# Making 22 products of the gate projections ahead of their phase, with four smaller edits, in a hybrid retention and attention layer

## The chip, the cores and the metric

One core of a Trainium2 chip runs the whole layer. The metric is device time in microseconds (us) of one execution; lower is better. TensorE (PE) multiplies matrices, VectorE (DVE), ScalarE (ACT) and GpSimd (POOL) work on tiles of 128 partitions, SyncE (SP) issues most of the DMAs. PSUM, where TensorE leaves its results, has eight banks of 512 fp32 numbers per partition.

## The reference

One layer over a sequence of 1024 tokens behind 16 meta tokens, width 1024, all in fp32:

```python
u = _rms_norm(h, pre_w)
z = u @ w_in                      # 60 column tiles of 128
rq, rk, rv, rg, aq, ak, av, ag, gr, ga = _split_in(z)
# branch A: 4 heads (key 128, value 256), chunks of 128, forward and backward scan
o_r = _bidirectional_retention(rot(rq), rot(rk), rv, lg_f, lg_b)
y_r = (group_norm(o_r) * ret_nw * silu(rg)) @ w_rb
# branch B: 8 heads in 2 groups, window of 128 to each side, 16 meta keys, one sink logit a head
#   m = max(max(s), sink); p = exp(s - m) / (sum(exp(s - m)) + exp(sink - m))
o_a = _windowed_sink_attention(rot(aq), rot(ak), av, sink)
y_a = (o_a * silu(ag)) @ w_ab
out = (sigmoid(gr) * y_r + sigmoid(ga) * y_a) @ w_o
return h + _rms_norm(out, post_w)
```

`rot` stands for the rotary positions, `lg_f` and `lg_b` for the logarithms of the decays. The four parts rg, ag, gr and ga are 32 column tiles, in the kernel 16 *gate units* of 256 columns.

## The kernel before

**Three matmuls for one.** Every fp32 product is made of three matmuls of a shorter format (`mm3`, L69 to L71: high by high, low by high, high by low). So each operand is split first: a copy in the short format is the high part (made by ScalarE, or by GpSimd through `pool_hi`, L74), and VectorE subtracts it for the low part (`dve_lo`, L77).

**Who sets the order.** The program is written stage by stage, with filler work between the steps of a stage. A scheduler then fixes, before the run, one order of instructions for each engine. It may lift an instruction over others that were written ahead of it, as far as its data and the buffers it takes allow; `tc.issue_after(x)` holds what is written under it behind x. Buffers come from pools in turn: a tag with n buffers hands out the next one only when the tile that had it n turns ago is done with. The tags of PSUM are `pj` (three banks, all projections), `p1` and `p2` (two each) and `p3` (one).

**The stages.**

1. *Retention* (`retention`, heads h = 0 to 3, up to about 330 us). Per head, a forward scan over chunks c = 0 to 8: `stage1` projects the values (`pv`), splits them and makes the scores, `stage2` adds up the outputs (`pa`) and the next state (`pkv`). Then a backward scan over c = 8 to 1: VectorE makes the next state `Sb`, GpSimd and VectorE split it (`Shb`, `Slb`), TensorE multiplies it with the queries (`pb`), VectorE adds this to the output `op`, normalises it (`bs`, `mv`, `rs`), and TensorE transposes it (`to`). In the backward scan each step calls `fill(KT)`, which draws eight pieces of filler; a piece is the three matmuls of one k of a projection. The filler of heads 0 to 2 is the next head's query and key projections (`gen_qk`), that of head 3 is the first keys and queries of the attention and one gate unit.
2. *Attention* (`attention`, pairs of heads hp = 0 to 3, about 330 to 590 us). Per block n of 128 queries: `stage1` makes the scores `ps` and the softmax, `stage2` transposes the probabilities `pt` and splits them, `stage3` multiplies with the values (`po`). Filler between the blocks, in amounts from the table `FILL`: the next queries, in pair 3 two gate units.
3. *Phases z, r, a, o* (`Phase`, `run`; from 589 us to the end). Four large products in Strassen's form as Winograd has it: a unit of 256 columns takes seven products in place of eight, each of 12 matmuls of 512 columns (`PROD`); sums of them give the four quarters of the unit (`POST`, `combine`). Phase z makes the gate units, r and a the two branch projections, o the output. The operands of a product are prepared six jobs ahead (`LEAD = 6`). The PSUM bank of a product goes by the table `at`: products 1, 6, 7 and 4 of a unit go one after the other through one bank X, which ScalarE copies out after each (`c1`, `u2`, `u3`), 5 and 3 share Y, 2 has Z. While a phase ends, hooks (`refill`) load and split the other operand of the next phase. Phase o ends in `last_product` and `o_tail`: the last addition, the square, the mean's power (on GpSimd) and the scaling of the last rows.

Three gate units (5, 6, 7 of `gr`) are made whole, with eight products' worth of matmuls, as filler by `gen_gate` (`N_GATE = 3`); the other 13 in phase z.

In the attention, the query block is split per block of 128 columns, high part on GpSimd. The sink enters the softmax's denominator by three small steps on a tile `es` (add, exponential, add). The values of a group are split per pair of heads, though two pairs share a group. `sums_of_x` makes differences of blocks of the normalised input, for phase z's operands T1 to T4, during pair 0, in a pool of its own. `x_to_out` copies six blocks of 128 rows of x to the output through on-chip memory, after pair 0; phase o adds to them.

Of the kernel before, what the change touches and what calls it, by code (L numbers as in the profile page):

```python
# [25 lines left out]
FILL = {**{h: (8, 8, 0, 8, 8, 8, 8, 0) for h in range(3)}, 3: (16, 16, 0, 16, 14, 10, 8, 0)}  # L26
N_GATE = 3
# [11 lines left out]
def block_kernel(ctx: ExitStack, tc: tile.TileContext, xT, x, w_in, w_rb, w_ab, w_out, vecs, dec, sink,  # L39
# [22 lines left out]

    xs_d = {n: dram.tile([4, P, 512], F32, tag=f"xs{n}", name=f"xs{n}") for n in ("T1", "T2", "T3", "T4")}
# [151 lines left out]
    def decay_table(hs):  # L215
        for h in hs:
            t = ra.tile([P, P], F32, tag="dd", bufs=2, name=f"dd{h}")
            nc.vector.tensor_scalar(t, tabt[:, 2 * P:3 * P], lg[:, 4 + h:5 + h], None, op0=ALU.mult)
            nc.vector.scalar_tensor_tensor(t, tabt[:, P:2 * P], lg[:, h:h + 1], t, op0=ALU.mult, op1=ALU.add)
            nc.scalar.activation(DT[:, h], t, AF.Exp)  # L220
# [211 lines left out]
    def retention(h, fill):  # L432
# [65 lines left out]
        def stage2(c):  # L498
# [11 lines left out]
            if "f" in kd:  # L510
                a, b = kd["f"]
                mm3(pk[:, 0:256], a[0:n], b[0:n], vh[0:n], vl[0:n], True, True)
# [104 lines left out]
    aq = {}  # L617

    wq = {}
# [37 lines left out]
    def sums_of_x(pool):  # L657

        x = {}

        def load(k):
            for i, j in ((0, 0), (0, 1), (1, 1), (1, 0)):
                x[k, i, j] = t = pool.tile([P, 512], F32, tag="xs", bufs=11, name=f"xs{i}{j}{k}")
                nc.sync.dma_start(t, xT[4 * i + k, :, NM + 512 * j:NM + 512 * j + 512])

        def make(k):
            for i, j in ((0, 0), (0, 1), (1, 1), (1, 0)):
                t = x[k, i, j]
                nc.scalar.activation(t, t, AF.Copy, scale=vec[:, 4 * i + k:4 * i + k + 1])
            for n, o, a, b in SUMS:  # L670
                nc.vector.tensor_tensor(x[k, *o], x[k, *a], x[k, *b], ALU.subtract)

        def store(k):
            for n, o, a, b in SUMS:
                nc.sync.dma_start(xs_d[n][k], x[k, *o])

        load(0)
        for k in range(6):
            if k < 3:
                load(k + 1)  # L680
            if k < 4:
                make(k)
            if 0 < k < 5:
                store(k - 1)
            yield
# [15 lines left out]
    def gen_gate(u):  # L701

        w = load_w(w_in, U_GR + u)
        for a, b in HALVES:
            for e_ in range(2):
                t = yield from proj(w, P * e_, a, b, f"pgt{u}_{a}{e_}")
                o = ra.tile([P, 512], F32, tag="m1", bufs=2, name=f"gt{u}_{a}{e_}")
                nc.vector.tensor_tensor(o, t, rbc[:, a:b], ALU.mult)
                nc.scalar.activation(o, o, AF.Tanh, scale=0.5)
                nc.sync.dma_start(tg_d[2 * u + e_, :, a - NM:b - NM], o)  # L710
                yield
# [5 lines left out]
    for h in range(NH):  # L717
        fill, drain = filler([*([gen_qk(h + 1)] if h < 3 else [gen_ak(0), gen_aq(0, 0), gen_gate(7)])])
# [4 lines left out]
        with tc.issue_after(rotated):  # L723
            retention(h, fill)
            drain()
# [29 lines left out]
    class Phase:  # L755
        def __init__(self, nm, seq, load, post, fetch=None, apart=(), early=()):
            self.nm, self.seq, self.load, self.post, self.fetch = nm, seq, load, post, fetch
            self.apart, self.early = apart, early
            self.raw, self.s, self.ops, self.u = {}, {}, {}, {}
            self.cur = None  # L760
# [18 lines left out]
        def prepare(self, u, p):  # L779
# [4 lines left out]
            if self.fetch and p in POST and u not in self.early:  # L784
                self.fetch(u, *POST[p])
# [11 lines left out]
            elif p == 6:  # L797
                t = self.s[u]
                self.split(u, 6, t)
                if u in self.early:  # L800
# [12 lines left out]
        def product(self, u, p):  # L813
# [3 lines left out]
            at = {1: "X", 6: "X", 7: "W" if u in self.apart else "X", 5: "Y", 3: "V" if u in self.early else "Y", 2: "Z",  # L817
# [26 lines left out]
        def combine(self, u, p, st):  # L844
# [15 lines left out]
            if p == 1:  # L860
                copy("c1")
            elif p == 2:
                self.post(u, 0, 0, plus(st["c1"], st["c1"], "Z"))
                done("Z")
            elif p == 6:
                copy("u2")
                if apart:
# [6 lines left out]
            elif p == 7 and not apart:  # L874
                copy("u3")
                if (self.nm, u) == last[:2]:
                    done("X")
            elif p == 3 and not early:
# [8 lines left out]
            if "u3" in st and "Y" in st and "c22" not in st:  # L887
                st["c22"] = plus(new("c5") if (self.nm, u) == last[:2] else st["u3"], st["u3"], "Y")
                self.post(u, 1, 1, st["c22"])
                if early:  # L890
# [21 lines left out]
    def refill(nm, src):  # L912
# [40 lines left out]

        if nm == "a":
# [157 lines left out]
    def o_tail(o, a):  # L1112
# [4 lines left out]
        if a:  # L1117
# [4 lines left out]
    seq += [(2, 1), (2, 5), (3, 1), (2, 6), (3, 5), (2, 2), (2, 7), (3, 6), (2, 4), (3, 7), (2, 3), (3, 2), (3, 3),  # L1122
            (3, 4)]
    gates = [U_G + u for u in range(4)] + [U_AG + u for u in range(4)] + [U_GR + u for u in range(8)]
    ph_o = Phase("o", seq, o_load, o_post, apart=(0, 1))
    steps = run([(Phase("z", sequence(16 - N_GATE, (1, 3, 2, 5, 6, 7, 4)), w_loader(w_in, gates), z_post, z_fetch,
                        early=(0, 1)),
# [6 lines left out]
    a_stack = ExitStack()  # L1134
    ap = a_stack.enter_context(tc.tile_pool(name="ap", bufs=1, reuse_waits="tile"))
# [18 lines left out]
    scored, softmax = [], []  # L1154

    def attention(hp, fill):
# [3 lines left out]
        vs = {}  # L1160
        oa = [None]
        st1, st2 = {}, {}

        def vsplit(b):
            a_ = ap.tile([P, P], R, tag="vh", bufs=4, name=f"vh{hp}_{b}")
            b_ = ap.tile([P, P], R, tag="vl", bufs=4, name=f"vl{hp}_{b}")
# [5 lines left out]
        def stage1(n):  # L1172
# [18 lines left out]
            es = ap.tile([P, 2], F32, tag="es", bufs=3, name=f"es{hp}_{n}")  # L1191
            pt = []
            for e_ in range(2):
                hd = 2 * hp + e_
                qr = aq[hp][e_, i][:, o0:o0 + P]
# [232 lines left out]
```

## Time and profile before

| | |
|---|---|
| time, median of 3 runs | 1092.71 us (1090.38 to 1093.98) |
| profiled execution | 1091.82 us, its span 1089.8 us |
| mean granted TensorE clock | 0.995 |
| TensorE (PE) busy | 1068.6 us, 98% of the span |
| TensorE's weight loads (PEld) | 922.5 us, 85%, beside the matmuls |
| VectorE (DVE) busy | 872.3 us, 80% |
| ScalarE (ACT) busy | 488.6 us, 45% |
| GpSimd (POOL) busy | 241.7 us, 22% |
| DMA | 159.45 MB, mean 146 GB/s |

"Busy" is time in which at least one instruction of the engine runs. Matmuls overlap, so a busy TensorE isn't one at its peak, and the count of matmuls in a stretch says more than its busy time. The granted clock is the share of its full speed that the throttle gave TensorE. In the rows below, "L69" is a line of the code, `pb<-Shb,qh` the tile written and the tiles read, by the names of the program; a row of a timeline has the start in us from the begin of the span, then the duration in us; a row of the groups has the count, the busy time in us and the mean of one in ns, then the idle time ahead of them with what ended it; a row of the stretches has for each engine the busy us and the number of instructions.

### The profile page before, as it was taken

The numbers are of one execution on the slowest core, as the hardware profiler recorded it, in microseconds if no ns is written. First come the engines' busy times: TensorE is split into PE (matmuls) and PEld (weight loads), VectorE is DVE, ScalarE is ACT, GpSimd is POOL, SyncE is SP. The second block draws the span as 40 slices with busy tenths as digits, with TensorE's granted clock in tenths as the row PEclk, the third lists the DMA queues.
The fourth block names the chain that finished last, engine by engine and source line by source line (L and its number), as shares of the span: only waits on it lengthen the run. The fifth ranks groups of instructions, "written<-read, shape, count | busy, mean of one in ns | idle before, by whom it ended". The sixth has DMA issues, their size and how long they took to land.

```text
span 1089.8 us, 17221 instructions
## 1 busy us (share of the span) xinstructions
PE 1068.6 (98%) x5975; PEld 922.5 (85%) x5975; DVE 872.3 (80%) x1864; ACT 488.6 (45%) x1132; POOL 241.7 (22%) x346
## 2 busy tenths in 40 slices
PE   8999999999999999999999999999999999999996
PEld 7899999998989889988887888888888788787885
DVE  7897778877955988898667975888889899767765
ACT  7241432513314544545657643454456546433442
POOL 3235324233322544445220000000000000110032
PEclk9999999998999999999999999999999999999999
DMA  7121101111114871112115663779874755779463
GB/s 289 39 79 40 55 24 59 59 40 39 63 44 144 295 277 60 59 59 68 50 49 169 238 227 120 247 240 324 276 274 140 236 185 200 235 202 336 118 116 78
DMA packets 75799, 159.45 MB, mean 146 GB/s; under 512 B 8128, under 2 KB 19904, under 8 KB 74944
## 3 DMA queue, kind: packets, MB, share of 16 engines
q1 hardware_dynamic: 71824, 151.78, 40.4%
q0 software_dynamic: 3456, 6.29, 3.7%
q8 instruction: 47, 0.77, 0.3%
q10 hardware_dynamic: 432, 0.28, 0.1%
q14 instruction: 40, 0.33, 0.1%
HBM read 105.89 MB, written 52.43 MB: 145 GB/s over the span
## 4 chain that ended last, share of the span: by engine, by line
PE 86%; DVE 5%; issue 3%; DMA 3%; POOL 2%; ACT 1%; SPq 0%; POOLq 0%; DVEq 0%; ACTq 0%
PE bz L70 8%; PE bz L69 8%; PE bz L71 8%; PE pv L69 3%; PE pv L70 3%; PE pv L71 3%; PE br L70 2%; PE bo L70 2%; PE bo L69 2%; PE bo L71 2%; PE br L69 2%; PE br L71 2%; PE ba L70 2%; PE ba L71 2%; PE ba L69 2%
## 5 line engine op out<-in xcount | busy, mean ns | idle before, releaser
L1054 POOL DMA_DIRECT2D mx_d<-c1a x4 | 3.7, 918 | 391.5 <-DVE c1a L1045 391.5
L70 PE MATMUL bz<-big,llz 128*128 128x512 f32 x208 | 82.4, 396 | 0.0
L71 PE MATMUL bz<-big,lhz 128*128 128x512 f32 x208 | 81.9, 394 | 0.0
L69 PE MATMUL bz<-big,lhz 128*128 128x512 f32 x208 | 80.8, 394 | 0.0
L69 PE MATMUL pv<-wh,big 128*128 128x256 f32 x256 | 73.6, 288 | 1.3 <-DVE m_qk L162 1.3
L70 PE MATMUL pv<-wh,big 128*128 128x256 f32 x256 | 73.4, 287 | 0.0
L71 PE MATMUL pv<-wl,big 128*128 128x256 f32 x256 | 73.2, 286 | 0.0
L69 PE MATMUL bz<-T,lhz 128*128 128x512 f32 x156 | 61.6, 395 | 0.0
L70 PE MATMUL bz<-T,llz 128*128 128x512 f32 x156 | 61.5, 395 | 0.0
L71 PE MATMUL bz<-T,lhz 128*128 128x512 f32 x156 | 61.3, 394 | 0.0
L1205 ACT ACTIVATE p<-p,nm 128x400 f32<-128x400 f32 (+1 forms) x64 | 38.3, 598 | 44.0 <-DVE nm L1203 42.3
L77 DVE TENSOR_TENSOR wl<-wr,wh 128x1024 fp32r<-128x1024 f32 x34 | 47.4, 1398 | 4.6 <-POOL wh L74 4.4
L70 PE MATMUL paq<-big,wl 128*128 128x512 f32 x128 | 51.0, 398 | 0.0
L71 PE MATMUL paq<-big,wh 128*128 128x512 f32 x128 | 50.9, 398 | 0.0
L69 PE MATMUL paq<-big,wh 128*128 128x512 f32 x128 | 50.8, 397 | 0.1
L69 PEld LDWEIGHTS pv<-wh,big 128*128 128x128 f32 x256 | 48.9, 191 | 2.1 <-DVE m_qk L162 1.5
L1217 POOL TENSOR_SCALAR p<-p,den 128x400 f32<-128x400 f32 (+1 forms) x60 | 36.0, 610 | 63.9 <-DVE den L1211 52.0
L70 PEld LDWEIGHTS pv<-wh,big 128*128 128x128 f32 x256 | 48.9, 191 | 0.1
L71 PEld LDWEIGHTS pv<-wl,big 128*128 128x128 f32 x256 | 48.9, 191 | 0.0
L69 PEld LDWEIGHTS bz<-big,lhz 128*128 128x128 f32 x208 | 39.0, 188 | 9.4
L70 PEld LDWEIGHTS bz<-big,llz 128*128 128x128 f32 x208 | 39.1, 188 | 9.3 <-DVE llz L77 0.2
L71 PEld LDWEIGHTS bz<-big,lhz 128*128 128x128 f32 x208 | 39.2, 188 | 8.9
(616 smaller groups left out, 3641.0 us busy)
## 6 DMA issues: line engine op xcount, KB each, us to landing
wr<-in_w_in_dram SPq DMA_DIRECT2D x35, 512.0 KB, 3.6
wrz<-in_w_in_dram SPq DMA_DIRECT2D x28, 512.0 KB, 5.7
tg<-tg_d SPq DMA_DIRECT2D x32, 256.0 KB, 4.7
T<-preT SPq DMA_DIRECT2D x6, 1024.0 KB, 7.5
oTr_d<-ost SPq DMA_DIRECT2D x16, 256.0 KB, 2.1
xs<-in_xT_dram SPq DMA_DIRECT2D x16, 256.0 KB, 5.5
xsT<-xs SPq DMA_DIRECT2D x16, 256.0 KB, 5.7
oTa_d<-oa SPq DMA_DIRECT2D x16, 256.0 KB, 2.1
```

What stands on the lines that cost most here:

```text
L69: nc.tensor.matmul(o, ah, bh, start=first, stop=False, **kw)
L70: nc.tensor.matmul(o, al, bh, start=False, stop=False, **kw)
L71: return nc.tensor.matmul(o, ah, bl, start=False, stop=last, **kw).ins
L77: return nc.vector.tensor_tensor(o, i, hi.bitcast(F32), ALU.subtract).ins
L1054: nc.gpsimd.dma_start(d, to, accum_op=ALU.add)
L1205: nc.scalar.activation(p[:, 0:wid], p[:, 0:wid], AF.Exp, scale=-1.0, bias=nm_[:, e_:e_ + 1], accum_out=den[:, e_:e_ + 1])
L1217: nc.gpsimd.tensor_scalar(pt[e_][:, 0:wid], pt[e_][:, 0:wid], den[:, e_:e_ + 1], 1.0, op0=ALU.mult, op1=ALU.mult)
```

## The change

* **Gates.** `gen_gate` is gone: all 16 gate units are made in phase z with seven products. Of these, product 2 of units 2 to 15 and product 3 of units 8 to 15 are made ahead by `gen_pre` as filler, 22 products of 12 matmuls; the result goes to a tensor in memory (`e_d`), and phase z loads it and adds it (`pre=PRE`).
* **Where they stand.** 16 pieces in the forward scans of heads 1, 2 and 3 (4, 4, 8, by `between`, behind the first matmuls of the state), 16 in the filler of head 3, the other 56 in the filler of pair 3.
* **Attention.** The sink is column 0 of the score tile (`raw`, 401 wide), so that the exponential's own sum takes it in; the `es` steps are gone. Queries are split by halves of 512, on ScalarE and VectorE (`split_q`). Values are split once for two pairs.
* **Sums of x** are made in pairs 1 and 2 (`sum_row`), in the tiles that weights are loaded to (`wr`). x goes to the output from memory to memory, in three DMAs of 1 MB.
* **Phase z's hooks** stand at other places, since products 2 and 3 of the last units are not in its sequence. The bank X of most units now takes product 7 sooner behind 6.
* **The last products** of phase o: (3, 7) moves behind (3, 3), which gets a bank of its own, V.
* `decay_table` takes its tile from the tag `rw` instead of `dd`.

```diff
-FILL = {**{h: (8, 8, 0, 8, 8, 8, 8, 0) for h in range(3)}, 3: (16, 16, 0, 16, 14, 10, 8, 0)}
-N_GATE = 3
+FILL = {**{h: (8, 8, 0, 8, 8, 8, 8, 0) for h in range(3)}, 3: (16, 16, 0, 14, 10, 8, 8, 0)}
+PRE = {u: (2, 3) if u > 7 else (2,) for u in range(2, 16)}
...
     def stage2(c):
...
-                mm3(pk[:, 0:256], a[0:n], b[0:n], vh[0:n], vl[0:n], True, True)
+                forward = mm3(pk[:, 0:256], a[0:n], b[0:n], vh[0:n], vl[0:n], True, True)
+                if h and c < 4:
+                    with tc.issue_after(forward):
+                        between(h // 3 + 1)
...
+    def split_q(hp, e_, i):
+        o = aq[hp][e_, i]
+        h, l = (aw.tile([P, 512], R, tag=f"aq{t}", bufs=4, name=f"aq{t}{hp}_{i}{e_}") for t in "hl")
+        nc.scalar.copy(h, o)
+        dve_lo(l, o, h)
+        aqs[hp, e_, i] = h, l
...
+    def gen_pre(u):
+        g = nc.vector.tensor_tensor
+        n = P * len(PRE[u])
+        raw = [keep.tile([P, 4, 256], F32, tag="wr", bufs=2, name=f"we{u}_{j}") for j in range(len(PRE[u]))]
+        for j, t in enumerate(reversed(raw)):
+            nc.sync.dma_start(t[:, :, 0:n], w_in[gates[u], :, 4 - 4 * j:8 - 4 * j, 0:n])
+        t = raw[-1]
+        if n > P:
+            v = t[:, :, P:n]
+            g(v, raw[0][:, :, P:n], v, ALU.add)
+            g(v, v, raw[0][:, :, 0:P], ALU.subtract)
+            g(v, t[:, :, 0:P], v, ALU.subtract)
+        h = wp.tile([P, 4, 256], R, tag="wh", bufs=4, name=f"weh{u}")[:, :, 0:n]
+        l = wp.tile([P, 4, 256], R, tag="wl", bufs=4, name=f"wel{u}")[:, :, 0:n]
+        nc.scalar.copy(h, t[:, :, 0:n])
+        dve_lo(l, t[:, :, 0:n], h)
+        for p in PRE[u]:
+            b = pj(f"pe{u}_{p}")
+            m = slice(P * (p - 2), P * (p - 1))
+            c = slice(NM + 512 * (p - 2), NM + 512 * (p - 1))
+            for k in range(4):
+                mm3(b, h[:, k, m], l[:, k, m], xh[4 + k][:, c], xl[4 + k][:, c], k == 0, k == 3, True)
+                if k < 3:
+                    yield
+            o = ra.tile([P, 512], F32, tag=f"m{p - 1}", bufs=2, name=f"e{u}_{p}")
+            nc.scalar.copy(o, b)
+            nc.sync.dma_start(e_d[u, p], o)
+            yield
...
-        fill, drain = filler([*([gen_qk(h + 1)] if h < 3 else [gen_ak(0), gen_aq(0, 0), gen_gate(7)])])
+        fill, drain = filler([*([gen_qk(h + 1)] if h < 3 else [gen_ak(0), pieces(pre, 16), gen_aq(0, 0)])])
...
-            retention(h, fill)
+            retention(h, fill, filler([pieces(pre, (0, 4, 4, 8)[h])])[0])
...
     class Phase:
...
+            made = {1: 2, 6: 3}.get(p)
+            if made not in self.pre.get(u, ()):
+                made = None
...
+            if made:
+                self.e[u, made] = gtile(f"e{u}{made}")
+                nc.sync.dma_start(self.e[u, made], e_d[u, made])
...
             if p == 1:
                 copy("c1")
+                e = self.e.pop((u, 2), None)
+                if e is not None:
+                    nc.vector.tensor_tensor(st["c1"], st["c1"], e, add)
+                    self.post(u, 0, 0, st["c1"])
+            elif p == 6 and (u, 3) in self.e:
+                st["u2"] = new("u2")
+                plus(st["u2"], self.e.pop((u, 3)), "X")
+                self.post(u, 0, 1, plus(st["u2"], st["u2"], "Y"))
...
-    seq += [(2, 1), (2, 5), (3, 1), (2, 6), (3, 5), (2, 2), (2, 7), (3, 6), (2, 4), (3, 7), (2, 3), (3, 2), (3, 3),
+    seq += [(2, 1), (2, 5), (3, 1), (2, 6), (3, 5), (2, 2), (2, 7), (3, 6), (2, 4), (2, 3), (3, 2), (3, 3), (3, 7),
             (3, 4)]
...
     def attention(hp, fill):
...
-                p = ap.tile([P, 400], F32, tag="p", bufs=4, name=f"p{hd}_{n}")
-                nc.vector.tensor_tensor_reduce(p[:, 0:wid], s[:, 0:wid], mask[:, mo:mo + wid], -SCALE,
+                if n == 0:
+                    raw[e_] = aw.tile([P, 401], F32, tag=f"raw{e_}", bufs=1, name=f"raw{hd}")
+                    nc.vector.tensor_copy(raw[e_][:, 0:1], nsink[:, hd:hd + 1])
+                p = ap.tile([P, 401], F32, tag="p", bufs=4, name=f"p{hd}_{n}")
+                nc.vector.tensor_tensor_reduce(raw[e_][:, 1:1 + wid], s[:, 0:wid], mask[:, mo:mo + wid], -SCALE,
                                                nsink[:, hd:hd + 1], ALU.add, ALU.min, nm_[:, e_:e_ + 1])
...
-            nc.vector.tensor_tensor(es, nm_, sinkc[:, 2 * hp:2 * hp + 2], ALU.add)
-            nc.scalar.activation(es, es, AF.Exp)
-            nc.vector.tensor_tensor(den, den, es, ALU.add)
...
+            if hp in (1, 2) and n in (2, 5):
+                sum_row(2 * hp - 2 + n // 3)
...
+        with tc.issue_after(stored[0]):
+            for r in (0, 4, 6):
+                nc.sync.dma_start(out[P * r:P * r + 2 * P], x[P * r:P * r + 2 * P])
```

137 lines of the change are left out of this document (58 added, 79 removed).

## The prediction

> **What bounds the kernel now.** I read the page first, then the busy time by stretches, then the timelines of TensorE and VectorE around the passages from one retention head to the next, and the last microseconds.
>
> ```profile
> span 1089.8 us, 17221 instructions
> PE 1068.6 (98%) x5975; PEld 922.5 (85%) x5975; DVE 872.3 (80%) x1864; ACT 488.6 (45%) x1132; POOL 241.7 (22%) x346
> core 0: us, PE busy (x) PEld busy (x) DVE busy (x) ACT busy (x) POOL busy (x), PEclk, DMA share, GB/s
> 630.00:660.00 30.00, 30.00 (x131) 24.29 (x130) 22.73 (x37) 14.82 (x26) 0.00 (x0) 1.00 0.61 207
> 107.00:122.00 15.00, 14.50 (x124) 14.21 (x122) 10.76 (x34) 4.99 (x18) 5.27 (x10) 1.00 0.11 37
> 255.00:260.00 5.00, 3.08 (x19) 2.20 (x18) 4.57 (x16) 2.11 (x7) 2.34 (x4) 0.93 0.17 56
> 260.00:266.00 6.00, 6.00 (x28) 5.59 (x27) 4.88 (x15) 2.47 (x8) 1.14 (x3) 0.50 0.14 45
> ```
>
> TensorE is the bound nearly everywhere. Its matmuls overlap, so their listed durations say nothing of the pace; the count does: 131 matmuls of 512 columns in 30 us are 0.229 us each. Time goes only where TensorE gets less work, or where it is made to wait. The one large hole in the middle is at 255 to 266 us (head 2 to head 3 of the retention): 19 matmuls in 5 us, then 28 in 6 us at a granted clock of 0.50. The two other passages look like the 107 to 122 row: 124 matmuls, full.
>
> **Part 1, TensorE work removed.** Before, three gate units are made whole: 3 units x 4 tiles x 8 x 3 = 288 matmuls, and 13 units x 7 products x 12 = 1092 in the Strassen-like phase z. After, all 16 units take 7 products: 1344, of which 22 products (264 matmuls) are made early and 90 products stay in phase z. That is 36 fewer, at 0.229 us: **-8.2 us**. All are full-pace matmuls in stretches where TensorE is the bound, so this is real if nothing else moves.
>
> **Part 2, the passages between retention heads.** This decides. I compared the compiled order of instructions of the two kernels on each engine.
>
> ```profile
> 103.46 0.28 PE L69 MATMUL pb<-Shb,qh 128*128 128x256 f32 x1
> 106.77 0.28 PE L69 MATMUL pb<-Shb,qh 128*128 128x256 f32 x1
> 120.07 0.28 PE L69 MATMUL pb<-Shb,qh 128*128 128x256 f32 x1
> 121.01 0.38 PE L555 MATMUL to<-ident,op 128*128 128x128 f32 x2
> 122.59 0.38 PE L69 MATMUL pkv<-vh,khf 16*128 16x256 f32 x1
> 124.74 0.39 PE L69 MATMUL pv<-wh,big 128*128 128x256 f32 x1
> 255.40 0.28 PE L69 MATMUL pb<-Shb,qh 128*128 128x256 f32 x1
> 256.59 0.36 PE L69 MATMUL pb<-Shb,qh 128*128 128x256 f32 x1
> 260.19 0.58 PE L69 MATMUL pkv<-vh,khf 16*128 16x256 f32 x1
> 263.32 0.41 PE L69 MATMUL pv<-wh,big 128*128 128x256 f32 x1
> ```
>
> The rows pb are steps of the backward scan, pkv is the first state of the next head's forward scan. In the old order the value projections pv_2 to pv_6 of head 1 (5 x 24 = 120 matmuls) stand between the steps pb_6 (103.46) and pb_1 (120.07); between 103.46 and 106.77 are 28 matmuls, 0.118 us each, so the cover is 14.2 us. In the new order they are gone from there. The early product `pe` takes its PSUM bank (tag `pj`, three banks) in the program just ahead of pv_2 and is tied behind the first pkv, and the scheduler no longer lifts pv_2 and what follows over it: after pv_1 come pb_5, to_8, pb_4, pb_3, to_7 and so on to tr_1, pkv_0, pe, and only then pv_2. So the five last backward steps run bare.
>
> How long they take is VectorE's affair:
>
> ```profile
> 105.80 0.41 DVE L77 TENSOR_TENSOR Slb<-Sb,Shb 128x256 fp32r<-128x256 f32 x1
> 112.17 0.41 DVE L77 TENSOR_TENSOR Slb<-Sb,Shb 128x256 fp32r<-128x256 f32 x1
> 112.50 0.17 DVE L584 BATCH_NORM_AGGREGATE mv<-bs 128x2 f32<-128x6 f32 x1
> L583 DVE BATCH_NORM_STATS2 bs<-op 128x6 f32<-128x256 f32 x32 | 13.4, 420 | 0.3
> L579 DVE SCALAR_TENSOR_TENSOR op<-pb,qd,op 128x256 f32<-128x256 f32 x28 | 13.4, 478 | 16.2 <-PE pb L71 15.9
> L587 DVE TENSOR_SCALAR op<-op,mv,rs 128x256 f32<-128x256 f32 x32 | 13.0, 405 | 0.6 <-POOL rs L586 0.4
> L77 DVE TENSOR_TENSOR ql<-qr,qh 128x512 fp32r<-128x512 f32 x8 | 5.4, 675 | 0.0
> ```
>
> pb_5 needs the split state that VectorE ends at 105.80 + 0.41 = 106.2. From there to the first klf, which pkv_0 needs, the new VectorE order has 1 vl, 6 bs, 5 op, 3 Slb, 2 Sb, 2 ql, 6 aggregates, 6 rs and 7 normalisations. By listed durations (I take 0.41 to 0.48 for each of 256 columns, 0.68 for ql, 0.17 for the small) that is about 14 us; but a 0.41 us operation lets the next start after 0.33 (112.17 to 112.50), and by such spacings it is 10.7 us. I take 11 with a wait or two: pkv_0 at about 118 instead of 122.59. TensorE comes to it 4.6 us sooner, but owes 14.2 us: 9.6 us lost. After pkv_0 the old order has a thin stretch to 124.74 which `pe` and pv_2 now fill, about 0.9 us: **+8.7 us**. This is not won back: those projections now cover the forward scan, but there the old kernel had its key projections lifted as cover, and no hole was left to fill.
>
> Then the clock. In the stretch 255 to 260 TensorE was 62% busy, never idle for long, and 260 to 266 ran at 0.50. The bare steps after pb_6 leave it about 25% busy for 12 us, so I expect a half-clock stretch reaching past pkv_0; the old one lost about 3 us of a 6.8 us stretch. **+3 us** (0 to 6).
>
> The Trainium skill, "TensorE: Matmul & The Clock Gate", section on what actually happens, has the clock fall only after an idle window of some 3.4 us. No gap in 255 to 260 is that long and the clock fell all the same, so this trace speaks for a fall at partial activity; by the page's rule the sum would lack these 3 us and those of the next passages.
>
> Heads 1 to 2: the new order covers all but the last two steps (to_5, 2 pv, pb_2, to_4, pb_1, to_3, tr), which is the old order at heads 2 to 3, whose 255.40 to 260.19 is 4.8 us with 14 matmuls (1.5 us): 3.3 us lost, plus half of a half-clock stretch (1.7), against the old 121.01 to 124.74, 3.7 us with 18 (2.0): 1.7. **+3.3 us**. Heads 2 to 3: the same 5.0 against the old one, where 47 matmuls worth 5.2 us took the 11 us of the two rows: **-0.8 us**. Part 2 together: **+14.2 us** (5 to 20; the low end is rival one plus noise).
>
> **Part 3, attention.** The query splits by halves, the sink column and the values split once take away:
>
> ```profile
> L77 DVE TENSOR_TENSOR aql<-aq,aqh 128x128 fp32r<-128x128 f32 x64 | 24.2, 392 | 6.2 <-POOL aqh L74 5.5
> L74 POOL TENSOR_SCALAR aqh<-aq 128x128 fp32r<-128x128 f32 x64 | 23.8, 378 | 26.8 <-PE ps L71 26.7
> L1210 DVE TENSOR_TENSOR den<-den,es 128x2 f32<-128x2 f32 x32 | 8.4, 262 | 3.3 <-ACT es L1209 3.1
> 570.00:580.00 10.00, 9.42 (x58) 8.05 (x57) 7.08 (x25) 8.05 (x24) 2.07 (x5) 1.00 0.16 55
> ```
>
> 24.2 + 8.4 us of VectorE and more go, but TensorE does not wait for them: at most 2 to 3 us of small holes can close. Against it, in the new order the early products run in the last blocks of pair 2 and the first of pair 3, four blocks of pair 3 stand without filler, and their weights need both raw buffers per unit. Blocks without filler are seen at 570 to 580: TensorE 9.42 of 10, so 0.3 to 0.4 us a block, 1.5 us for four. The sums of x move under pairs 1 and 2, whose VectorE has just been relieved, and hold the raw weight buffers, which are loaded long ahead; the copy of x to the output goes from memory to memory on SP's queue while DMA is light. **+1.5 us** (-3 to +7).
>
> **Part 4, phase z.** One product fewer is counted. Added are 22 loads and 22 stores of 256 KB, 22 additions, 12 more outputs to scale.
>
> ```profile
> 730.00:740.00 10.00, 10.00 (x45) 8.11 (x44) 10.00 (x18) 5.15 (x9) 0.00 (x0) 1.00 0.99 341
> 790.00:800.00 10.00, 10.00 (x45) 8.11 (x44) 6.02 (x10) 4.64 (x9) 0.00 (x0) 1.00 1.01 373
> 863.30 0.59 ACT L850 COPY u2r<-br 128x512 f32<-128x512 f32 x1 [4.93 <-DMA tg_d<-u2z]
> ```
>
> TensorE stays full in stretches where DMA is at 1.0 of its share and VectorE at 10 of 10, so there is slack, and the work lies six products (16.5 us) ahead. What loses its slack: with product 2 gone, product 7 follows 6 in the same PSUM bank after one other product (12 x 0.229 = 2.75 us) instead of three, and ScalarE must have copied the bank by then. The copy takes 0.59 us, but the row at 863.30 shows one that came 4.9 us into an idle ScalarE held by another wait. Nothing to 12 us; I take **+2 us**.
>
> **Part 5, the end.** Product (3,7) moves next to last, so that row 2 is ready sooner.
>
> ```profile
> 1081.22 0.42 DVE L841 TENSOR_TENSOR u3o<-u3o,bo 128x256 f32<-128x256 f32 x1 [0.73 <-PE bo L71]
> 1082.00 0.19 ACT L1094 ACTIVATION_READ_ACCUMULATOR jk<-u3o 128x1 f32 x1
> 1082.97 0.75 DVE L1106 SCALAR_TENSOR_TENSOR c1o<-c1o,ms,xres 128x512 f32<-128x512 f32 x1
> 1084.30 0.15 DVE L1099 SCALAR_TENSOR_TENSOR ms<-ms,ms 128x1 f32<-128x1 f32 x1
> 1085.11 0.75 DVE L1106 SCALAR_TENSOR_TENSOR c5o<-c5o,ms,xres 128x512 f32<-128x512 f32 x1 [0.66 <-POOL ms L1103]
> ```
>
> ScalarE has the last square at 1082.19, but the step ms that takes it comes at 1084.30, behind row 2's scaling on VectorE. In the new order row 2 stands ahead of the last addition, so ms can go at about 1082.4: **-1.8 us** (0 to -2.2). What is late next is GpSimd's power, then the same two scalings.
>
> **The sum.** The profiled execution took 1091.8 us (span 1089.8 and 2.0 around it), 0.9 under the median of the runs. -8.2 + 14.2 + 1.5 + 2 - 1.8 = +7.7: **1099 us**.
>
> **Rivals.** *One, faster:* the bare steps follow one another not at VectorE's 2 us but at the 1.2 us seen between 255.40 and 256.59. Then pb_1 is at 106.2 + 4 x 1.2 = 111, pkv_0 3.6 us later (256.59 to 260.19) at 114.6, the loss 14.2 - 8.0 - 0.9 = 5.3 us; with the clock kept and the other passages at +1.6 and -2.5, part 2 is +4.4, and with attention and z at nothing the time is 1091.8 - 8.2 - 1.8 + 4.4 = 1086. It decides if pkv_0 comes before 115. Against it: at 255 two states had been made ahead, and five steps use that up. Chance 0.18.
>
> *Two, no change:* the clock stays at 1.0 through all passages because TensorE does something every 2 us. Part 2 is then 8.7 + 1.6 - 2.5 = 7.8, the time 1093. The section of the page named above would have it so. The row 260 to 266 is against it. Chance 0.12.
>
> *Three, much slower:* in phase z the copy between products 6 and 7 comes late once a unit. 14 units x 0.7 us are 10 us more than nothing, 1107 to 1110. Chance 0.15. For it: ScalarE's splits wait in order behind DMAs. Against: most copies start at once.
>
> **How the numbers follow.** Forecast 0.55, its own spread 1093 to 1106. About 0.3% (3.3 us, 1089.4 to 1096.0) is what a measurement can tell from no change. Faster: rival one with 0.17, a little of the others: 0.20. Within: rival two, the low end of the forecast: 0.19. Slower: the rest, 0.61. The range 1085 to 1110 leaves out the better half of rival one and the worst of rival three.
>
> **What would show it.** Right: near 104 to 118 us TensorE with under 40 matmuls in 14 us and a granted clock of 0.5 before 125; pkv_0 of head 1 near 118; retention ending some 13 us later; ms at the end within 1.5 us of the last addition. Wrong: those stretches full, or pkv_0 before 115; phase z longer than 90 x 2.75 us by more than 5.

## The result, and the profile after

| | before | after |
|---|---|---|
| time, median | 1092.91 us | 1122.41 us |
| ratio | | 1.0281, 95% interval 1.0259 to 1.0303 |
| span of the profiled execution | 1089.8 us | 1120.5 us |
| matmuls | 5975 | 5939 |
| mean granted clock | 0.995 | 0.978 |

The forecast was slower, by 6 to 7 us; measured were 29.5. From the page of the changed kernel (the span, the busy time of the engines, the row of the clock):

```profile
span 1120.5 us, 17075 instructions
PE 1077.5 (96%) x5939; PEld 924.8 (83%) x5939; DVE 887.9 (79%) x1797; ACT 510.3 (46%) x1128; POOL 217.9 (19%) x276
PEclk9999799898999999999999999999999999999998
```

36 matmuls fewer, and TensorE is *busy* 9 us longer, since matmuls at half clock last longer (0.55 us in place of 0.35 in the timeline below). The row of the clock shows where: in slices of 28 us, the fifth (112 to 140), the eighth and the tenth.

To see where 30.7 us of span come from I used one measure in every trace: from the start of one matmul to the next, less the lower quartile of that distance for matmuls of its shape in the kernel before (0.229 us for 512 columns, 0.117 for 256). What is left is the **excess**, time in which TensorE didn't go at its pace. Stages are cut at matmuls that both kernels have; each column has the excess in us.

| stage | before | after | difference |
|---|---|---|---|
| first state of head 0 to that of head 1 | 5.1 | 15.3 | +10.2 |
| head 1 to head 2 | 6.3 | 13.1 | +6.8 |
| head 2 to head 3 | 7.5 | 11.8 | +4.3 |
| head 3 to the attention | 6.7 | 7.4 | +0.7 |
| attention, pairs 0 and 1 | 10.1 | 7.0 | -3.1 |
| attention, pairs 2 and 3 | 11.9 | 20.1 | +8.2 |
| phase z | 2.7 | 9.2 | +6.5 |
| phase r | 1.2 | 7.2 | +6.0 |
| the rest (start, values, phases a and o) | 14.9 | 15.2 | +0.3 |

That is 39.9 us more excess. The 36 matmuls take 8.3 off, and from the last matmul to the end it is 7.9 us in place of 8.8: 39.9 - 8.3 - 0.9 = 30.7. Each excess comes from one profiled execution. For most versions below it lies within 2 us of the median time; where it lies further off, the text says so.

**The passages.** A passage is the change from one retention head to the next. Busy time by stretches around the first passage (104 to 125), the second and the third, in the changed kernel:

```profile
104.00:118.00 14.00, 7.74 (x30) 5.16 (x31) 13.31 (x46) 4.75 (x15) 7.92 (x13) 0.63 0.23 75
118.00:125.00 7.00, 7.00 (x30) 6.26 (x30) 1.84 (x6) 0.66 (x2) 0.48 (x1) 0.51 0.13 40
189.00:197.00 8.00, 4.24 (x21) 2.80 (x19) 6.79 (x24) 3.14 (x10) 2.36 (x4) 0.76 0.35 124
265.00:278.00 13.00, 9.55 (x44) 7.63 (x42) 8.85 (x28) 3.44 (x11) 3.25 (x6) 0.75 0.25 81
```

30 matmuls in 14 us where the kernel before had 124 in 15; VectorE 13.31 of 14 busy, and a granted clock of 0.63, then 0.51. The steps behind it, and those of the second passage, from the timeline:

```profile
103.15 0.28 PE L71 MATMUL pb<-Shb,qh 128*128 128x256 f32 x1
104.99 0.36 PE L71 MATMUL pb<-Shb,qh 128*128 128x256 f32 x1 [1.22 <-DVE rs L591]
107.10 0.35 PE L71 MATMUL pb<-Shb,qh 128*128 128x256 f32 x1 [1.29 <-DVE op L585]
109.49 0.55 PE L71 MATMUL pb<-Shb,qh 128*128 128x256 f32 x1 [1.80 <-DVE op L585]
111.32 0.55 PE L71 MATMUL pb<-Shb,qh 128*128 128x256 f32 x1
112.97 0.55 PE L71 MATMUL pb<-Shb,qh 128*128 128x256 f32 x1 [0.21 <-DVE rs L591]
118.45 0.58 PE L71 MATMUL pkv<-vh,khf 16*128 16x256 f32 x1
189.78 0.36 PE L71 MATMUL pb<-Shb,qh 128*128 128x256 f32 x1 [0.43 <-DVE op L585]
192.09 0.36 PE L71 MATMUL pb<-Shb,qh 128*128 128x256 f32 x1
196.39 0.58 PE L71 MATMUL pkv<-vh,khf 16*128 16x256 f32 x1
```

Five backward steps (the rows 104.99 to 112.97) without cover, each 1.65 to 2.4 us behind the step before it (not the 1.2 of rival one), and the next head's first state at 118.45 (forecast: 118). From 109.49 on the same matmul lasts 0.55 us in place of 0.35: the clock has fallen.

What is missing can be counted. The table has the matmuls of the value projections (`pv`) that start in the 18 us before each head's first state, and the excess from 18 us before that state to 12 us after it.

| passage | before: `pv` | after: `pv` | before: excess | after: excess |
|---|---|---|---|---|
| first | 114 | 23 | 4.5 | 16.0 |
| second | 114 | 40 | 4.3 | 10.5 |
| third | 92 | 40 | 8.3 | 9.2 |

**Phases z and r.** What TensorE waited for at 741 to 750, and at 878 to 890 (total, number and longest of the waits, in us); then the rows of three engines that lead to the first:

```profile
PE bz L71 <- ACT u3z L885: 2.2, 1, 2.2
PE br L72 <- DVE llr L79: 3.6, 2, 2.9
```

```profile
741.99 0.62 ACT L692 CAST wT11h<-w 128x512 fp32r<-128x512 f32 x1 [2.39 <-DVE w L690]
743.63 0.69 DVE L690 TENSOR_TENSOR w<-w,w 128x512 f32<-128x512 f32 x1 [1.07 <-DMA w<-in_w_out_dram]
744.35 0.62 ACT L692 CAST wT31h<-w 128x512 fp32r<-128x512 f32 x1 [1.74 <-DVE w L690]
744.88 0.58 ACT L885 COPY u3z<-bz 128x512 f32<-128x512 f32 x1
745.51 0.50 PE L71 MATMUL bz<-T,lhz 128*128 128x512 f32 x1 [2.20 <-ACT u3z L885]
```

Read upwards: TensorE needs bank X, which ScalarE frees with the copy `u3z` (L885). That copy stands behind `wT31h` (L692), which splits the last phase's weights and waits for VectorE, which waits for a DMA. DMA was full then: its share in 720 to 750 is 0.99.

```profile
720.00:750.00 30.00, 27.80 (x114) 22.11 (x113) 27.21 (x46) 14.99 (x27) 0.00 (x0) 0.94 0.99 339
840.00:870.00 30.00, 29.49 (x128) 23.59 (x127) 29.68 (x50) 17.08 (x32) 0.00 (x0) 1.00 0.54 174
870.00:900.00 30.00, 26.45 (x107) 20.75 (x106) 26.67 (x44) 16.65 (x30) 0.00 (x0) 0.94 0.64 224
```

The other hole (870 to 900) waits for another engine: VectorE has been busy 29.68 of 30 us just before, and is late with the low part `llr` of the next product's weights. A full VectorE alone makes no hole, though. In the kernel before it was as full, and TensorE lost nothing:

```profile
818.00:848.00 30.00, 30.00 (x131) 24.28 (x130) 30.00 (x51) 19.79 (x37) 0.00 (x0) 1.00 0.49 157
```

Behind each hole stands a 3.4 us stretch of half clock.

### The profile page after: what moved, and what is told of

Same layout as the page of the kernel before. It is cut to its first block, busy times and chain, and to the rows that moved or that the text cites. A ratio compares the mean times of both kernels' runs of the same rounds, so it can differ in the third digit from the quotient of the medians.

```text
span 1120.5 us, 17075 instructions
## 1 busy us (share of the span) xinstructions
PE 1077.5 (96%) x5939; PEld 924.8 (83%) x5939; DVE 887.9 (79%) x1797; ACT 510.3 (46%) x1128; POOL 217.9 (19%) x276
## 4 chain that ended last, share of the span: by engine, by line
PE 50%; DVE 13%; DMA 7%; issue 3%; ACT 3%; SPq 0%; DVEq 0%; POOL 0%; POOLq 0%; ACTq 0%
PE bz L71 4%; PE bz L72 4%; PE bz L73 4%; PE bo L72 2%; PE bo L71 2%; PE bo L73 2%; PE br L72 2%; PE br L73 2%; PE ba L72 2%; PE br L71 2%; PE ba L73 2%; PE ba L71 2%; PE paq L71 2%; PE paq L72 2%; PE paq L73 2%
## 5 line engine op out<-in xcount | busy, mean ns | idle before, releaser
L71 PE MATMUL bz<-T,lhz 128*128 128x512 f32 x192 | 76.6, 399 | 2.8 <-ACT u3z L885 2.2
L73 PE MATMUL bz<-T,lhz 128*128 128x512 f32 x192 | 76.3, 398 | 0.0
L72 PE MATMUL bz<-T,llz 128*128 128x512 f32 x192 | 76.2, 397 | 0.0
L72 PE MATMUL bz<-big,llz 128*128 128x512 f32 x168 | 66.7, 397 | 0.0
L71 PE MATMUL bz<-big,lhz 128*128 128x512 f32 x168 | 66.4, 399 | 0.0
L73 PE MATMUL bz<-big,lhz 128*128 128x512 f32 x168 | 66.3, 396 | 0.0
L1255 DVE CUSTOM_DVE_ANT_0 raw<-ps,mask,nsink 128x400 f32<-128x400 f32 (+1 forms) x64 | 37.9, 595 | 25.3 <-ACT p L1258 24.4
L71 PEld LDWEIGHTS pv<-wh,big 128*128 128x128 f32 x256 | 51.0, 199 | 2.2 <-DVE m_qk L164 1.5
L1258 ACT ACTIVATE p<-raw,nm 128x401 f32<-128x401 f32 (+1 forms) x64 | 38.8, 606 | 28.5 <-PE pt L1284 16.7
L72 PEld LDWEIGHTS pv<-wh,big 128*128 128x128 f32 x256 | 50.8, 198 | 0.8
L566 ACT ACTIVATE ost<-to,rnw 128x128 f32<-128x128 f32 x64 | 20.0, 364 | 61.9 <-PE to L561 56.9
L71 PEld LDWEIGHTS bz<-T,lhz 128*128 128x128 f32 x192 | 36.6, 190 | 12.0 <-ACT u3z L885 2.6
L72 PEld LDWEIGHTS bz<-T,llz 128*128 128x128 f32 x192 | 36.6, 191 | 8.5
```

What stands on the lines that cost most here:

```text
L71: nc.tensor.matmul(o, ah, bh, start=first, stop=False, **kw)
L72: nc.tensor.matmul(o, al, bh, start=False, stop=False, **kw)
L73: return nc.tensor.matmul(o, ah, bl, start=False, stop=last, **kw).ins
L566: nc.scalar.activation(ost[0][:, e_, w0:w0 + P], to[:, P * e_:P * e_ + P], AF.Copy, scale=rnw[:, 2 * h + e_:2 * h + e_ + 1])
L1255: nc.vector.tensor_tensor_reduce(raw[e_][:, 1:1 + wid], s[:, 0:wid], mask[:, mo:mo + wid], -SCALE, nsink[:, hd:hd + 1], ALU.add, ALU.min, ...
L1258: nc.scalar.activation(p[:, 0:1 + wid], raw[e_][:, 0:1 + wid], AF.Exp, scale=-1.0, bias=nm_[:, e_:e_ + 1], accum_out=den[:, e_:e_ + 1])
```

## The experiments

Ratios are to the kernel before, run on the same chip. The experiments ran on several chips, on which the kernel before has medians of 1092.4 to 1093.5 us, so two versions are best compared by their ratios.

**1. Without the hold** (all else as in the changed kernel):

```diff
-                    with tc.issue_after(forward):
-                        between(h // 3 + 1)
+                    between(h // 3 + 1)
```

> The changed kernel with one line less: the early products drawn behind the forward states are no longer held behind those states, all else as it is. Theory one (the hold, together with the PSUM bank taken in turn, keeps the next head's value projections from standing between the last backward steps): the matmuls of the passages are covered again, the excess of TensorE over its pace at 95 to 130, 180 to 212 and 255 to 285 us falls from 16.1, 10.6 and 9.2 us to about 4, 4 and 8 as before the change, the granted clock stays at 1.0 at the first two, and the time is 1122 - 20 = about 1102 us. Theory two (the bank alone, or VectorE's added work for the early products, makes the passages long): 1118 us or more, passages as they are.

1102.78 us, ratio 1.0100 (1.0083 to 1.0117). Its stretch of the first passage:

```profile
104.00:118.00 14.00, 14.00 (x111) 13.52 (x110) 12.42 (x36) 5.10 (x16) 7.76 (x11) 1.00 0.34 113
```

111 matmuls where the changed kernel has 30, clock 1.00. The value projections are back (117, 117 and 91 of their matmuls in the 18 us before the first states), and the excess of the three passages is 3.8, 4.3 and 4.3 us. That of the third is below the 8.3 from before the change: 12 matmuls of an early product were lifted into it. One line was 19.6 us.

**2. The pieces elsewhere** (16 from the forward scans to head 3's filler):

```diff
-        fill, drain = filler([*([gen_qk(h + 1)] if h < 3 else [gen_ak(0), pieces(pre, 16), gen_aq(0, 0)])])
+        fill, drain = filler([*([gen_qk(h + 1)] if h < 3 else [gen_ak(0), pieces(pre, 32), gen_aq(0, 0)])])
...
-            retention(h, fill, filler([pieces(pre, (0, 4, 4, 8)[h])])[0])
+            retention(h, fill, filler([])[0])
```

> The changed kernel with the 16 pieces of the forward scans moved into the filler of head 3 (32 pieces there in place of 16). Theory one (the pieces at that place cost the cover): passages as before the change, about 1102 us, and the same within 4 us as the kernel that only leaves out the hold. Theory two (VectorE and ScalarE work added elsewhere makes the passages long): above 1115 us.

1101.35 us, 1.0088 (1.0069 to 1.0106), with 114, 114 and 92 matmuls of the value projections and 4.5, 4.3 and 8.3 us of excess in the passages: just as before the change. Theory one in both.

**3. The hold, with a bank of its own:**

```diff
-    banks = {"pj": 3, "p1": 2, "p2": 2, "p3": 1}
+    banks = {"pj": 2, "pe": 1, "p1": 2, "p2": 2, "p3": 1}
...
-            b = pj(f"pe{u}_{p}")
+            b = pe_(f"pe{u}_{p}")
...
-    free = ["pj"] * 3
+    free = ["pj", "pj", "pe"]
```

> The changed kernel with the hold kept, but the early products take a PSUM bank of their own, and the projections have two banks in place of three. Theory one (the cover is lost because the held product stands in the turn of the banks that the value projections take; hold and shared bank are both needed): the compiled order has the value projections of the next head back between the backward steps, the passages lose 4 to 8 us each as before the change, and the time is about 1103 us, some us more if two banks hold up the projections elsewhere. Theory two (the hold alone orders the projections): passages of 16, 10 and 9 us, about 1122 us.

1105.97 us, 1.0123 (1.0104 to 1.0141), its profiled execution 2.4 us above that; 114, 116 and 116 matmuls of the value projections and 5.7, 3.8 and 3.0 us of excess in the passages. So the hold alone does not take the cover away: it is the held product *in the turn of the banks*, ahead of the projections that take the same banks, that keeps those from being lifted. Two banks for the projections cost some 5 to 7 us in the first 54 us: the excess there is 17.5 us, and 10.3 to 12.4 in all other versions.

**4. Two score tiles** for each head, so that VectorE's scores don't wait for ScalarE's exponential of the block before:

```diff
-                if n == 0:
-                    raw[e_] = aw.tile([P, 401], F32, tag=f"raw{e_}", bufs=1, name=f"raw{hd}")
+                if n < 2:
+                    raw[e_, n] = aw.tile([P, 401], F32, tag=f"raw{e_}", bufs=2, name=f"raw{hd}_{n}")
...
-                nc.scalar.activation(p[:, 0:1 + wid], raw[e_][:, 0:1 + wid], AF.Exp, scale=-1.0,
+                nc.scalar.activation(p[:, 0:1 + wid], raw[e_, n % 2][:, 0:1 + wid], AF.Exp, scale=-1.0,
...
```

> The changed kernel with two score tiles for each head of a pair in place of one, so that VectorE can take the scores of the next block while ScalarE still reads the last. Theory one (the single score tile ties VectorE's reading of the scores behind ScalarE's exponential, and TensorE behind that): the waits of the scores at 582 to 596 us (0.3 to 1.0 us each) go, 3 to 5 us less, about 1118 us. Theory two (blocks without filler are thin anyway, as before the change at 570 to 590): less than 1 us.

1123.13 us, 1.0289 (1.0274 to 1.0304): nothing. The wait that the trace puts on the scores was not what held the blocks.

**5. Early products of other units** (PRE: 2 of units 2 to 13, 3 of units 2 to 11; hooks where they stood before the change), with the hold, and then without:

> The changed kernel with the same number of early products, but of other units: product 2 of units 2 to 13 and product 3 of units 2 to 11, so that units 14 and 15 have all seven products in phase z, and the loads and splits for the next phase stand where they stood before the change. Theory one (with products 2 and 3 gone from the last units, VectorE has the same work for fewer products at the end of phase z, and comes late by the 4.9 us seen at 880 to 890): that hole goes, 1122 - 5 = about 1117 us. Theory two (the hole comes from the loads' order, or from the DMAs, not from VectorE): hole stays, 1121 to 1124 us.

1121.31 us, 1.0273 (1.0258 to 1.0287). The hole of phase r shrank (7.2 to 2.6 us), but the time by 1.1 us only.

> The kernel without the hold, with the early products taken from other units (2 of units 2 to 13, 3 of units 2 to 11) and the steps for the next phase where they stood before the change. With the hold this took the excess at the start of phase r from 7.2 to 2.6 us, though the time fell by 1.1 us only, since other stretches took back 3 us. Theory one (those 3 us are chance of another order and the hole is VectorE's load per product): 1102.8 - 4.5 = about 1098 us. Theory two (what is won there is given back elsewhere in phase z): 1101 to 1103 us.

1100.09 us, 1.0068 (1.0045 to 1.0091), against 1102.78 (1.0100): about 3 us, between the two theories. Phase z fell from 12.1 to 6.8 and r from 6.8 to 2.7 us of excess, and head 2's scan took 4.6 back.

**6. The last phase's weights prepared earlier** (on the kernel without the hold):

```diff
-        hooks[10 * k + 30] = [lambda k=k: pre_split(k, stage, act_src(w_out))]
+        hooks[10 * k + 8] = [lambda k=k: pre_split(k, stage, act_src(w_out))]
```

> The kernel without the hold, with the four steps that prepare the last phase's operand from memory moved 22 products ahead in phase z (after products 8, 18, 28, 38 in place of 30, 40, 50, 60). Theory one (where the early products are loaded, DMA is full, 0.94 of its share; these steps wait there for their loads, and ScalarE, which takes its work in order, comes late to the copy that frees the bank): the hole of 2.2 us and the half clock behind it go, excess of phase z from 12.1 to about 6 us, the time from 1102.8 to about 1098 us. Theory two (the copies come late because products 6 and 7 of a unit stand closer, wherever the steps are): the hole moves or stays, 1102 us.

1095.42 us, 1.0025 (1.0010 to 1.0040): 7.4 us off by the medians, 8.2 by the ratios, more than expected. The hole at the copy went (z 8.7 us of excess in place of 12.1), and the one of phase r with it (2.3 in place of 6.8). Products 6 and 7 stand as close as they did, so their distance alone makes no hole. Before, two of the four steps stood among the products of units 8 to 15 (from product 50 on), for which two early results a unit are loaded; now all four stand ahead of them. DMA is as full as it was, and TensorE makes its 131 matmuls:

```profile
720.00:750.00 30.00, 30.00 (x131) 24.32 (x130) 27.99 (x48) 16.04 (x29) 0.00 (x0) 1.00 0.99 348
```

So a full DMA alone doesn't make the hole; with the rows of the trace above it is the step on ScalarE that waits for its load in front of the copy. A smaller excess of 1.9 us is left at 747 to 757.

**7. All filler that there is, in pair 3** (no pieces in the forward scans, 72 in pair 3, 16 in head 3):

```diff
-FILL = {**{h: (8, 8, 0, 8, 8, 8, 8, 0) for h in range(3)}, 3: (16, 16, 0, 14, 10, 8, 8, 0)}
+FILL = {**{h: (8, 8, 0, 8, 8, 8, 8, 0) for h in range(3)}, 3: (16, 16, 8, 16, 14, 10, 8, 0)}
...
-            retention(h, fill, filler([pieces(pre, (0, 4, 4, 8)[h])])[0])
+            retention(h, fill, filler([])[0])
```

> The changed kernel with no early pieces in the forward scans; they are drawn in pair 3, which takes 72 in place of 56 (the table of its filler is raised by 16 pieces to 88, the filler of head 3 stays at 16). In the compiled order two blocks of pair 3 stand without filler in place of four. Theory one (the attention lost time because it has less filler than the gate units made whole gave it): against the kernel that puts these 16 pieces into head 3 (1101.4 us) the excess of pair 3 falls from 12.7 us to about 8, and the time to about 1097 us. Theory two (the last blocks are thin by their own chain of softmax and transposes, whatever fills the others): within 1.5 us of 1101.

1095.90 us, 1.0023 (1.0010 to 1.0037): the time that theory one gave, but not by its mechanism. The excess of pair 3 didn't fall (15.1 us in place of 12.7, in a pair that is longer now). The scheduler lifts the pieces: 87 matmuls of early products start at 480 to 520, in pair 2, and none in the last 7 us of pair 3, which is bare again. Pair 2 (8.3 to 5.2) and head 3 (6.6 to 4.1) have less excess. Where the 5.5 us of the medians come from is not shown, since this version's profiled execution lies 4.6 us above its median and has the same excess in all as that of experiment 2 (84.6 and 84.9 us).

**8. Where the bare blocks stand.** Edit 6 and 7 together are the best version (below). On it, pair 3's filler was held behind the scores of the next block, from block 2 on and from block 4 on:

```diff
-            if hp < 3 or n < NB - 2:
+            if hp < 3 or n < 2:
                 fill(FILL[hp][n])
+            elif n < NB - 2:
+                with tc.issue_after(scored[-1]):
+                    fill(FILL[hp][n])
```

> The best version so far (no early pieces in the forward scans, 72 in pair 3, the steps for the last phase earlier), with the filler of pair 3 from block 2 on held behind the scores of the following block, so that it can't be lifted ahead. In the compiled order the last blocks of pair 3 then have filler each, and four blocks at the turn from pair 2 to pair 3 stand bare in their place. Theory one (a bare block costs most at the end of the attention, where ScalarE also scales the probabilities and copies for phase z): excess from pair 2 to the first product of phase z and the 11.4 us behind it together fall by 4 us or more, to about 1086 us. Theory two (a bare block costs the same wherever it stands, and there are as many): within 1 us of 1090.4. Theory three (where pieces are held, the order behind them gets worse, as in the retention): 1093 us or more.

> As the last, with the filler held from block 4 of pair 3 on only; the bare blocks then stand in the middle of pair 3. Theory one: 2 to 4 us less than 1090.4; theory two: the same; theory three: 1092 us or more.

1095.64 us (1.0031, 1.0019 to 1.0043) and 1094.36 us (1.0008, 0.9995 to 1.0021), against 1090.36 (0.9984) without the holds. By the ratios that is 5 and 2.6 us slower, which is theory three; theory one is refuted. The holes moved, as the order said: 15.5 us of excess at 500 to 530 in the first, 12.4 at 530 to 560 in the second, each with two half-clock stretches. The whole excess of the profiles is nearly the same (78.0 without holds; 79.0; 78.6 us), as theory two had it; but the profiled execution without the holds was the slowest of its twelve (1093.82 us), 3.5 above the median, so this doesn't show that a bare block costs the same anywhere. Why the holds cost time isn't explained.

**9. Gates whole again, all other edits kept** (13 units in phase z, `gen_gate` as filler, no early products):

> The changed kernel with three gate units made whole as before the change, 13 in phase z, no early products, and phase z's steps where they stood; all other edits stay (attention, sums of x, last products, copy of x). Theory one (the early products cost all of the loss, the other edits gain a little: 3.1 us of excess in pair 0, some 0.5 us at the end): about 1089 us. Theory two (the attention edits cost time in pairs 2 and 3, whose excess went from 4.7 and 7.2 to 7.6 and 12.6 us): 1094 to 1098 us.

1092.95 us, 1.0008 (0.9999 to 1.0016), between the theories. By the medians the early products, with the way they were placed, are the whole loss, and the other edits come to nothing in sum. The profile has them win 3.1 us in pair 0 (6.0 to 2.9) and lose 6.5 in pair 3 and phase z (9.9 to 16.4). Up to 3.4 of the 6.5 are a half-clock stretch of 6.83 us at 586.2, which the kernel before doesn't have there; the rest is open.

**10. The last products alone,** on the kernel before:

> The kernel before with the last products reordered and nothing else. Theory one (the step from the last matmul to the end shortens by 1.8 us, as forecast): 1090.8 us. Theory two (only by the 0.9 to 1.2 us seen in the changed kernel, 8.85 to 7.95 us, and the phase itself takes 0.7 us more): within 1 us of before.

1091.51 us, 0.9991 (0.9982 to 1.0000), 1.2 us less, with an interval that reaches to no change: between the theories.

**11. The best version:** edits 6 and 7 on the changed kernel; and the same with the pieces left in the forward scans without the hold, and none in head 3.

> The two edits that gained most, together: no early pieces in the forward scans and 72 in pair 3, and the steps that prepare the last phase's operand 22 products earlier. Theory one (the losses are separate and add): 1095.9 less the 7.4 us that the second edit took off without the first, about 1089 us, 3 us faster than before the change, with an excess of phases z and r of 8.7 and 2.3 us. Theory two (blocks of pair 3 without filler and the end of attention hold the rest): 1092 to 1095 us.

1090.36 us, 0.9984 (0.9974 to 0.9994): 1.7 us faster than the kernel before by the ratio, 2.3 by the medians, the one version whose interval stays below 1. The two savings don't quite add (1089 expected).

> As the last, but the 16 pieces of the forward scans stay there without the hold, and those of head 3's filler go to pair 3. Theory one (pieces without the hold are lifted to the passages and cover them, 4.4 us of excess at 250 to 280 in place of 8.4): 1 to 2 us less than the last, about 1088 us. Theory two (head 3 then lacks filler): 1091 us or more.

1095.80 us, 1.0029 (1.0018 to 1.0040): the time that theory two gave. But head 3 and what follows it up to the attention have only 1.6 us more excess; pairs 0 and 1 have 4.9 more (11.6 in place of 6.8), and why those is not shown (this profiled execution lies 2.6 us above the median).

## Why the prediction was wrong in size

The sum said +7.7 us, the span grew by 30.7. Of the 23 us between them, part 4 has 10.5, part 2 has 7.8, part 3 has 3.6 and part 5 has 1.2. The first bare passage, which the prediction worked out in full, came as it said; the largest part of the miss is in waits of phases z and r, which it had at +2.

**Part 1, held by count, not as a saving.** 36 matmuls went, 8.3 us. But the gate units made whole had been *cover*: 96 pieces of filler in head 3 and pair 3, where 80 remain (16 + 8 in head 3, 56 in pair 3). 16 pieces are 48 matmuls, 11 us of cover. The step took full-pace matmuls for pure cost. Where TensorE would wait for a chain of other engines anyway, part of them cost nothing, and taking them away saves nothing. What this was worth isn't measured by itself: with the gate units back (experiment 9) pairs 2 and 3 have 16.1 us of excess in place of 20.1.

**Part 2, right in mechanism, too small.** Forecast +14.2, measured +22.0 by stage. The first passage is as worked out: +11.5 us of excess against 8.7 + 3. The failing term is the second passage (+3.3 forecast, +6.2 measured): I took its length from the old passage of heads 2 to 3, whose state chain was further ahead; from pb_2 (189.78) to the first state (196.39) it took 6.6 us, not 4.8. And the half clock, by the trace's record of the granted clock, lasted 17.1 us at the first passage (107.8 to 124.8) and 10.2 at the second (193.1 to 203.3), where I had allowed 6.8 and half of that. At the first this changed little, since only the 6.4 us from 118.45 on had dense matmuls to slow down, with 2.9 us of excess for the 3 forecast: the cost came out right by luck, with a length that was wrong. At the second the dense 7.0 us from 196.39 on have 3.1 us of excess, where I had 1.7. The third passage is +1.0 (9.2 against 8.3) where -0.8 was forecast. The other 3 us stand in the scans between the passages, about 1 us in each scan that takes early pieces; I had put nothing there. Experiments 1 to 3 show hold and bank together as the cause in the passages.

The clock fell at 107.8 us. The Trainium skill, "TensorE: Matmul & The Clock Gate", section "What's actually happening", lets it fall after an idle window of some 3.4 us. No distance between the starts of matmuls in the 4 us up to and across that moment was over 2.1 us (107.41 to 109.49), so here too it fell without an empty window; rival two, which went by that rule, is refuted. The lengths do fit: the stretches of half clock up to the last matmul last 3.41, 6.83, 10.24 and 17.07 us, multiples of the window of 3413 ns that the same section of the Trainium skill gives.

**Part 3, inside its bounds, mis-sized.** +5.1 for +1.5 (bounds -3 to +7). Pair 0 gained 3.1, somewhat more than I had for the closed holes; it did so though 12.1 of the 24.2 us of VectorE's low parts of the queries stay, which I had counted as gone. Pairs 2 and 3 lost 8.2. The price of a bare block, 0.3 to 0.4 us, was read from the wrong column: I took TensorE's busy share at 570 to 580 (9.42 of 10), though busy time says nothing of the pace. By the measure used here the excess of that very stretch is 2.05 us, and 3.07 in the ten us behind it. Four bare blocks at such a price would be several us. How much of the 8.2 they are is open: of the 5.3 us in pair 3, 3.7 stay when the gate units are back (experiment 9), part of them with the clock that falls there.

**Part 4, the largest failing step.** +2 forecast for phase z (0 to 12), +12.5 measured in z and r; some 2 us of it are the attention's last chains, which reach into phase z. Rival three named the wait (a late copy of bank X, ScalarE's order behind a DMA), but as 0.7 us in 14 units; it came once, 2.2 us and a half-clock stretch. The hole of phase r, 3.6 us of waits and another such stretch, was a term put at nothing: I saw slack in a TensorE that stayed full at 10 of 10 of VectorE, but with fewer products per unit the same sums and splits come in less time. Two experiments bear on it. With early products of other units the hole of phase r shrinks from 7.2 to 2.6 us (experiment 5), and experiment 6 takes 8 us out of z and r with the place of four steps alone. How far DMA and VectorE each carry it isn't told apart.

**Part 5, the chain right, the end not.** -1.8 forecast, -0.9 measured from the last matmul to the end, and phase o gave most of that back. From the start of the last addition to that of the last scaling:

```profile
1081.22 0.42 DVE L841 TENSOR_TENSOR u3o<-u3o,bo 128x256 f32<-128x256 f32 x1 [0.73 <-PE bo L71]
1085.78 0.75 DVE L1106 SCALAR_TENSOR_TENSOR u3o<-u3o,ms,xres 128x512 f32<-128x512 f32 x1
```

before, 4.6 us, and after

```profile
1113.54 0.41 DVE L876 TENSOR_TENSOR u3o<-u3o,bo 128x256 f32<-128x256 f32 x1
1114.52 0.16 DVE L1151 SCALAR_TENSOR_TENSOR ms<-ms,ms 128x1 f32<-128x1 f32 x1 [0.17 <-ACT jk L1146]
1116.13 0.75 DVE L1158 SCALAR_TENSOR_TENSOR u3o<-u3o,ms,xres 128x512 f32<-128x512 f32 x1
```

2.6 us: 2.0 less, for 1.8 forecast, and ms comes 1.0 us behind the addition. But the addition itself comes 1.0 us after the last matmul begins (1112.55) in place of 0.3 (1080.90), VectorE being busy, and phase o has 0.7 us more excess.

## What to carry to other kernels

Before a new piece of work goes into a schedule, look at what it is tied to *and* what stands behind it in the turn of the buffers it takes: an instruction held in place, in a shared pool, holds all later users of the pool too. Work that fills a chain's gaps costs less than its own time, so count cover lost apart from work removed. Price a bare stretch by the pace of its matmuls, not by busy time, and add the slower clock behind it. When a phase gets shorter, look for the fixed work in it (loads, splits, copies for the next phase): it must fit into fewer products.

## What the hardware showed that was not expected

TensorE's clock halved at 107.8 us in a stretch where a matmul began at least every 2.1 us, and stayed at half for 6.4 us after matmuls were dense again (118.45 to 124.84). A single wait of TensorE of 2.2 us in phase z, with no excess to speak of in the 6 us before 741, was followed by a half-clock stretch of 3.4 us that began 0.6 us after the wait.
